# The delta rule's block products on one NeuronCore: 64x64 tiles against full 128x128 products over zero-padded operands

## The chip, the cores and the metric

The kernel runs on one core of a Trainium2 chip, as one program. The metric is the device time of one execution in microseconds; smaller is better. Times named here are medians of several executions, or parts of one profiled execution. The engines are called as the profile calls them: PE (TensorE, the matmuls), PEld (its weight loads), DVE (VectorE), ACT (ScalarE), POOL (GpSimd) and SP (SyncE, whose queue issues the DMAs here).

## What is computed

One layer of a streaming encoder over 2048 tokens of width 1024, in float32. One large input projection feeds two branches, a gated spatial mixing (group A) and a gated DeltaNet (group B) of 8 heads of width 128. Both go through one output projection, and a gated per-layer embedding follows. The part that matters here is the delta rule of group B, worked out in chunks of 64 tokens:

```python
def chunk_gated_delta_rule(q, k, v, g, beta):      # C = 64 tokens in a chunk
    ...
    A = where(strict, einsum('bhnik,bhnjk->bhnij', k_beta, k) * L, 0.0)
    T = triangular_solve(A + eye, eye)             # inverse of a 64x64 lower triangle
    u = einsum('bhnij,bhnjv->bhniv', T, v * beta[..., None])
    w = einsum('bhnij,bhnjk->bhnik', T, k_beta * exp(decay)[..., None])
    qk = einsum('bhnik,bhnjk->bhnij', q, k) * L
    ...
    def step(state, inp):                          # one chunk after another
        v_new = u_c - w_c @ state
        o_c = q_c @ state + qk_c @ v_new
        state = state * a_c + k_c.T @ v_new
        return state, o_c
```

## The kernel before

The tokens run in two passes of 1024. In each pass the projections are a stream of 128x512 products, each done as three float32r passes over operands split into a high and a low part (`mm3`). Everything else is woven into this stream by hand: an object `Flow` keeps an estimated time, and small tasks (generators) emit their instructions between the products of the stream when their estimates say that their inputs are ready. The result is one fixed order of instructions on each engine. `Flow` books a small float32 product by its moving width alone (`mm`), so its estimate is the same for 64 and for 128 partitions.

Group B goes head by head, 8 heads in each pass, numbered 0 to 15 in the text. A pair of two 64-token chunks stands on the 128 partitions, and is called a unit here; a head in a pass has 8 units in two blocks of 4. For each head and pass there are three stages.

- `front` builds the matrix `AT` (what `A` is in the reference, transposed) and `QK` from the products `pkq`, and writes the two diagonal 64x64 blocks of `AT` to DRAM (`atd`).
- `inverse` loads them in another layout (`ain`) and inverts all sixteen 64x64 triangles of a head at once on GpSimd, by 63 steps of a multiply (`xtmp`) and a subtract (`xs`). The result goes to DRAM (`td`) and comes back as `Dt`, in two DMAs (`d` = 0 and 1), one for each half of the partitions.
- `chain` walks through the 8 units. Each unit solves with the inverses in `Dt` in three products: the upper half (`Dt`), the coupling from the upper to the lower half (`AT`), and the lower half (`Dt`). These three are called block products here. Before the change they are on 64 partitions and 64 columns. Around them stand `pc<-S,kq`, `pc<-w,kd` and two `po` products, which are 128x128. `r`, `x1` and `w` are the steps between the products, on DVE, ACT and DVE.

`finish` closes each block of four units: its sum of squares `sso` goes to DVE and then, as a power, to GpSimd, in the same queue as the steps of the next head's inversion. There are two such instructions for each head.

All DMAs are issued by SP in one order. PE takes its instructions in order too, so a product that waits holds up everything behind it.

Of the kernel before, what the change touches and what calls it, by code (L numbers as in the profile page):

```python
"""Hybrid gMLP + gated DeltaNet trunk layer, float32, on one core.

Large products run as three float32r passes over operands split exactly into a
high and a low part; the delta rule, the spatial mixing and the transposes run
in plain float32.
"""
# [1 line left out]

# [11 lines left out]
P = 128  # L20
# [8 lines left out]


class Flow:
    """Emission order: a stream of large products with latency-bound work woven in.

    Times are estimates in nanoseconds; they only decide the order in which
    each engine's instructions are issued.
    """

    def __init__(self):
        self.t = 0.0
# [61 lines left out]
def trunk(tc, a, out):  # L101
# [67 lines left out]
    with ExitStack() as outer:  # L169
# [164 lines left out]
                fl.used["kq"] -= 4  # L334

        def inv_rms(xs):
            """1 / rms of every token, along the free axis on all partitions."""
            dg = gt("xs", "dg", [P, 4, P], 1)
            for i, (xt,) in enumerate(xs):
                yield from fl.room("act")  # L340
                yield from fl.take("acc")
                fl.give("acc")
                junk = gt("acc", "junk", [P, D], 3, BF16)
                ss = gt("ss1", "ss1", [P, 2], 4)
                r, f = rstd_of(gp, ss[:, :1], D, "rs1", act(junk, xt, AF.Square, accum_out=ss[:, :1]))
                yield f
                f = ts(dg[:, i], ident, r, None, ALU.mult, after=f)
            fl.used["kq"] -= 4
            yield f + 2000
            rb = bank("ch", "rb", [P, 512])  # L350
            f = mm(rb, ones, dg.rearrange("p a b -> p (a b)"), True, True)
            yield f
            return rb
# [39 lines left out]
            return ps  # L393

        def proj_both(X, ui, c, mid):
            """Both blocks share the pass over X, which frees its first parts sooner."""
            banks = []
            for b in range(2):
                yield pj_free
                fl.used["pj"] = fl.used.get("pj", 0) + 1  # L400
                banks.append(bank("pj", "pj", [P, 512]))
            cc = slice(c * P, c * P + P)
            for k in range(NK):
                hi, lo = W[ui, k // 2]
                for b in range(2):
                    yield from mm3(banks[b], hi[:, k % 2, cc], lo[:, k % 2, cc], X[k][0][:, b], X[k][1][:, b],
                                   k == 0, k == NK - 1)
                if k % 2:
                    fl.give("w")
                mid[k]()  # L410
            return banks
# [58 lines left out]
                fl.spawn(scalars(ab), 9000, 3)  # L470

        def v_unit(X, p, ui, n, stats):
            """Token major products; several token tiles share the pass over the weights."""
            fetch(ui + 1)
            rest = rest_w(ui + 1)
            ab = gt("ab", "ab", [P, 16, 8], 1) if n == 0 else None
            w = 256 if n else 272
            if n:
                groups = [((0, 1), "pj"), ((2, 3), "m"), ((4, 5), "pj"), ((6, 7), "m")]
            elif p == 0:  # L480
                groups = [((0, 1, 2, 3), "pm"), ((4, 5, 6, 7), "pm")]
            else:
                groups = [((0, 1, 2, 3), "pm"), ((4, 5), "pj"), ((6, 7), "m")]
            for group, where in groups:
                banks = []
                for i, t in enumerate(group):
                    tag = ("pj", "m")[i // 2] if where == "pm" else where
                    yield fl.free(tag)
                    fl.used[tag] = fl.used.get(tag, 0) + 1
                    banks.append((t, tag, bank(tag, "pv", [P, 512])))  # L490
                for k in range(NK):
                    if p == 0 and n == 0:
                        yield lambda: xready[group[0] // 4] > k
                    yield lambda: len(X) > k and (ui, k // 2) in W
                    hi, lo = W[ui, k // 2]
                    for t, tag, ps in banks:
                        tk = slice((t % 4) * P, (t % 4) * P + P)
                        yield from mm3(ps[:, :w], X[k][0][:, t // 4, tk], X[k][1][:, t // 4, tk],
                                       hi[:, k % 2, :w], lo[:, k % 2, :w], k == 0, k == NK - 1)
                    if group[-1] == 7:  # L500
                        if k % 2:
                            fl.give("w")
                        if k in rest:
                            rest[k]()
                for t, tag, ps in banks:
                    fl.spawn(v_post(p, ps, t, n, stats, ab, tag), 170, 1)
                if 3 in group:
                    next_w(ui + 1, 0)
# [160 lines left out]
            return f  # L669

        def decay(p, h, b, i):
            """exp of the summed decays between two tokens, zero above the diagonal, transposed."""
            beta, gh, gl, ex, ne = SC[p]
            cs = slice(h * 8 + b * 4, h * 8 + b * 4 + 4)
            while len(fronts) < i + b - 1 or len(Ls) < i + b:
                yield fl.t + 300
            R = []
            for gg in (gh, gl):
                yield from fl.take("R")
                yield from fl.room("pool", 800)  # L680
                r = gt("R", "R", [P, 4, P], 2, F32R)
                f = asel(r, gg[:, cs, None].bitcast(F32).to_broadcast([P, 4, P]))
                R.append(r)
            yield f
            yield from fl.take("m")
            pd = bank("m", "pd")
            mm(pd, mgt_r, R[0], True, False)
            f = mm(pd, mgt_r, R[1], False, True)
            fl.give("R")
            fl.give("R")  # L690
            yield f
            yield from fl.room("act")
            L = gt("L", "L", [P, 4, P], 2)
            f = act(L, pd, AF.Exp, after=f)
            fl.give("m")
            yield asel(L, L, after=f)
            Ls.append(L)
# [93 lines left out]
        def inverse(p, h, st):  # L791
# [31 lines left out]
            yield fl.t + 2600  # L823
            while len(done) < st["i"]:
                yield fl.t + 300
            Dt = gt("Dt", "Dt", [P, 8, 64], 1)
            for d in range(2):
                dma(Dt[d * 64:d * 64 + 64], td.rearrange("c (u d) i -> d c u i", d=2)[d])
            fl.spawn(chain(p, h, st, Dt), 4500, 0)

        def chain(p, h, st, Dt):
            beta, gh, gl, ex, ne = SC[p]
            while len(done) < st["i"] or len(st["R"]) < 2:
                yield fl.t + 300
# [1 line left out]
            for b in range(2):  # L836
# [4 lines left out]
                for u in range(4):  # L841
# [9 lines left out]
                        r = gt("r", "r", [P, P], 1)  # L851
                        yield stt(r, pc[:, 0], ne[:, cu], vn[:, u], ALU.mult, ALU.add, after=f)
                    po = bank("o", "po", [P, 2, P])
                    f = mm(pc[0:64, 1], Dt[0:64, b * 4 + u, :], r[0:64], True, True)
                    x1 = gt("x1", "x1", [64, P], 1)
                    fx = act(x1, pc[0:64, 1], AF.Copy, after=f)
                    if not first:
                        f = mm(po[:, 0], kq[:, u, 1, :], Sp, True, True)
                        oe = gt("oe", "oe", [P, P], 1)
                        fo = act(oe, po[:, 0], AF.Copy, scale=ex[:, 0, cu], after=f)  # L860
                    yield fx
                    f = mm(pc[64:128, 2], AT[0:64, u, 64:128], x1, True, True)
                    yield tt(r[64:128], r[64:128], pc[64:128, 2], ALU.subtract, after=f)
                    f = mm(pc[64:128, 1], Dt[64:128, b * 4 + u, :], r[64:128], True, True)
                    w = gt("w", "w", [P, P], 1)
                    yield ts(w, pc[:, 1], bn[:, u:u + 1], None, ALU.mult, after=f)
                    fs = 0
# [9 lines left out]
                    if first:  # L877
                        f = vcopy(ot[:, u], po[:, 1], after=f)
                    else:
                        f = tt(ot[:, u], oe, po[:, 1], ALU.add, after=max(f, fo))  # L880
                    junk = gt("junkc", "junkc", [P, P], 2, BF16)
                    f = act(junk, ot[:, u], AF.Square, accum_out=sso[:, u:u + 1], after=f)
                    yield fs
                fl.give("kq")
# [28 lines left out]
            tt(lo, src, hi.bitcast(F32), ALU.subtract)  # L913

        def stage(pool, j, name, loads, staged):
            """Two half tiles of 512 columns each, from the slots that are free by then."""
            if pool is gp and j % 3 == 2:
                tiles = []
                for _ in range(2):
# [16 lines left out]
            staged[j] = tiles  # L936

        def refill(pool, free, sources, sink, name):
            """Split operands into the resident slots as the products before release them."""
            n = len(sources)  # L940
            staged = {}
            for j in range(min(3, n)):
# [321 lines left out]
        nega = const("alog", [P, NH])  # L1264
        mgt_r = cp.tile([P, P], F32R, name="mgt_r")
        X0 = x_tiles()

        def setup():
            act(nega, nega, AF.Exp)
            ts(nega, nega, -1.0, None, ALU.mult)  # L1270
            act(mgt_r, mgt, AF.Copy)
# [72 lines left out]
```

## Time and profile before

| | us |
|---|---|
| median of 3 runs | 2430.47 |
| lowest and highest | 2428.53 and 2433.29 |
| span of the profiled execution | 2427.2 |
| PE busy in it | 2366.6 (98%) |
| GpSimd (POOL) busy in it | 1106.8 (46%) |
| DVE busy, ACT busy | 1310.7 (54%), 1023.5 (42%) |

The span runs from the first to the last instruction of the profiled execution, whose own whole time is not told apart from it; the median of the timed runs is 3.3 us above the span. A busy PE is not a PE at its peak: a product is counted from its start to its modelled end, and these overlap, so the distance from one start to the next tells more than a duration. A float32 product is shown as two passes.

### The profile page before, as it was taken

How to read it: one execution, taken by the hardware profiler on the slowest of the kernel's cores; microseconds unless marked ns; L12 is line 12 of the kernel's file. 1: busy time of each engine (PE TensorE's matmuls, PEld its weight loads, DVE VectorE, ACT ScalarE, POOL GpSimd, SP SyncE). 2: the span in 40 equal slices, each digit the busy share in tenths (PEclk: the TensorE clock that was granted, in tenths of full speed). 3: DMA queues.
4: the chain of work that ended last, by engine and by line, in shares of the span. 5: the costliest groups of instructions: out<-in, count | busy, mean ns of one | idle time of the engine just before them, and what ended most of it. 6: DMA issues, size and time to landing. Idle time of an engine off the chain costs nothing.

```text
span 2427.2 us, 34751 instructions
## 1 busy us (share of the span) xinstructions
PE 2366.6 (98%) x11884; PEld 1853.0 (76%) x11884; DVE 1310.7 (54%) x2843; ACT 1023.5 (42%) x2410; POOL 1106.8 (46%) x2246
## 2 busy tenths in 40 slices
PE   8999999999999999999999999999999999999998
PEld 8987677777776778987777676777766887887886
DVE  5456465565664754356556475564664334346665
ACT  5544354443543543444344353443532223234443
POOL 1128558567585681046757567576670000001111
PEclk9999999999999999999999999999999999999999
DMA  6532332223322242232232232322253457452221
GB/s 203 208 115 73 88 88 78 80 75 96 89 71 82 81 151 91 78 90 72 79 89 66 82 88 74 89 77 87 86 172 115 139 166 228 139 176 89 79 82 62
DMA packets 249201, 253.22 MB, mean 104 GB/s; under 512 B 66112, under 2 KB 163904, under 8 KB 249024
## 3 DMA queue, kind: packets, MB, share of 16 engines
q1 hardware_dynamic: 249024, 251.01, 33.1%
q8 instruction: 93, 1.52, 0.3%
q14 instruction: 84, 0.69, 0.1%
HBM read 195.89 MB, written 55.05 MB: 103 GB/s over the span
## 4 chain that ended last, share of the span: by engine, by line
PE 53%; POOL 31%; issue 6%; DMA 5%; DVE 2%; ACT 1%; SPq 0%; POOLq 0%; DVEq 0%; ACTq 0%
PE pj L115 16%; POOL xs L162 14%; POOL xtmp L162 13%; PE pso L115 12%; PE pg L115 7%; PE pv L115 7%; PE pc L115 5%; PE po L115 2%; PE pe L115 2%; POOL R L166 2%; DMA Dt<-td 1%; PE pkq L115 1%; DMA ain<-atd 1%; DMA td<-xs 1%; POOL sso L158 1%
## 5 line engine op out<-in xcount | busy, mean ns | idle before, releaser
L162 POOL TENSOR_TENSOR xtmp<-ain,xs 128x132 f32<-128x132 f32 (+47 forms) x1008 | 453.7, 450 | 344.8 <-DMA ain<-atd 260.8
L162 POOL TENSOR_TENSOR xs<-xs,xtmp 128x132 f32<-128x132 f32 (+47 forms) x1008 | 473.9, 470 | 79.0
L115 PE MATMUL pj<-xrhi,whi 128*128 128x512 f32 x768 | 314.5, 410 | 0.0
L115 PE MATMUL pj<-xhi,wlo 128*128 128x512 f32 x768 | 314.2, 409 | 0.0
L115 PE MATMUL pj<-xrhi,wlo 128*128 128x512 f32 x768 | 313.5, 408 | 0.0
L115 PE MATMUL pj<-xhi,whi 128*128 128x512 f32 x768 | 312.9, 407 | 0.0
L115 PE MATMUL pj<-xrlo,whi 128*128 128x512 f32 x768 | 312.5, 407 | 0.0
L115 PE MATMUL pj<-xlo,whi 128*128 128x512 f32 x768 | 311.2, 405 | 0.0
L158 POOL TENSOR_TENSOR rstd<-rstd,nhalf 128x1 f32<-128x1 f32 x64 | 42.9, 677 | 578.8 <-DVE rstd L146 578.8
L139 DVE SCALAR_TENSOR_TENSOR acc<-pre,cw,acc 128x512 f32<-128x512 f32 x288 | 226.4, 786 | 26.1 <-ACT acc L126 21.9
L115 PE MATMUL pso<-wohi,ylo 128*128 128x512 f32 x512 | 205.7, 402 | 0.0
L115 PE MATMUL pso<-wolo,yhi 128*128 128x512 f32 x512 | 204.5, 399 | 0.8 <-DVE wolo L135 0.7
L115 PE MATMUL pso<-wohi,yhi 128*128 128x512 f32 x512 | 202.5, 395 | 0.0
L135 DVE TENSOR_TENSOR wlo<-raw,whi 128x512 fp32r<-128x512 f32 x224 | 163.8, 734 | 63.5 <-ACT whi L126 60.6
L126 ACT ACTIVATE yhi<-yraw 128x512 fp32r<-128x512 f32 x128 | 80.2, 629 | 220.2 <-PE pso L115 216.3
L115 PEld LDWEIGHTS pj<-xhi,wlo 128*128 128x128 f32 x768 | 145.3, 189 | 31.9 <-issue 7.0
L115 PEld LDWEIGHTS pj<-xrhi,whi 128*128 128x128 f32 x768 | 145.6, 190 | 31.5 <-issue 7.5
L115 PEld LDWEIGHTS pj<-xhi,whi 128*128 128x128 f32 x768 | 145.5, 189 | 31.0 <-issue 6.9
L115 PEld LDWEIGHTS pj<-xrlo,whi 128*128 128x128 f32 x768 | 145.5, 189 | 30.4 <-issue 6.3
L115 PEld LDWEIGHTS pj<-xlo,whi 128*128 128x128 f32 x768 | 145.3, 189 | 30.7 <-issue 5.3
L115 PEld LDWEIGHTS pj<-xrhi,wlo 128*128 128x128 f32 x768 | 145.7, 190 | 29.5 <-issue 4.6
L126 ACT ACTIVATE junkc<-ot 128x128 bf16<-128x128 f32 x128 | 39.7, 310 | 302.9 <-DVE ot L135 283.7
(200 smaller groups left out, 4893.7 us busy)
## 6 DMA issues: line engine op xcount, KB each, us to landing
raw<-in_wu SPq DMA_DIRECT2D x224, 256.0 KB
ain<-atd SPq DMA_DIRECT2D x128, 256.0 KB
yraw<-ysc SPq DMA_DIRECT2D x128, 256.0 KB
vsc<-gv SPq DMA_DIRECT2D x64, 128.0 KB
gn<-vsc SPq DMA_DIRECT2D x32, 256.0 KB
ysc<-gn SPq DMA_DIRECT2D x32, 256.0 KB
ysc<-zb SPq DMA_DIRECT2D x32, 256.0 KB
wo<-in_wo SPq DMA_DIRECT2D x32, 256.0 KB
```

The costliest lines, as they stand in the source:

```text
L115: nc.tensor.matmul(o, lhsT, rhs, start=start, stop=stop)
L126: nc.scalar.activation(o, i, func, **kw)
L135: nc.vector.tensor_tensor(o, x, y, op)
L139: nc.vector.scalar_tensor_tensor(o, x, sc, y, op0, op1)
L158: nc.gpsimd.tensor_tensor(o, x, y, ALU.pow)
L162: nc.gpsimd.tensor_tensor(o, x, y, op)
L166: nc.gpsimd.affine_select(o, x, [[0, 4], [1, P]], ALU.is_ge, 0.0, 0, -1)
```

## The change

The three block products become full 128x128 products. `Dt` is now one tile of [128, 8, 128], made once and zeroed once; the DMAs fill only its two diagonal 64x64 blocks, so the off-diagonal blocks stay zero. `x1` is likewise one [128, 128] tile whose lower half stays zero. The first and the third block product both write all 128 rows of `pc[:, 1]`. Of the first, ACT uses only the upper half; the third gives both halves again, from the corrected `r`. The product with `AT` takes the whole matrix, and its lower half is used. Two scratch tiles are dropped: `oe`, whose content goes straight to `ot`, and `junkc`, which shares `junk`. The zeroing is two DVE instructions in `setup`.

```diff
         def inverse(p, h, st):
...
-            Dt = gt("Dt", "Dt", [P, 8, 64], 1)
             for d in range(2):
-                dma(Dt[d * 64:d * 64 + 64], td.rearrange("c (u d) i -> d c u i", d=2)[d])
-            fl.spawn(chain(p, h, st, Dt), 4500, 0)
+                dd = slice(d * 64, d * 64 + 64)
+                dma(Dt[dd, :, dd], td.rearrange("c (u d) i -> d c u i", d=2)[d])
+            fl.spawn(chain(p, h, st), 4500, 0)
...
                     po = bank("o", "po", [P, 2, P])
-                    f = mm(pc[0:64, 1], Dt[0:64, b * 4 + u, :], r[0:64], True, True)
-                    x1 = gt("x1", "x1", [64, P], 1)
-                    fx = act(x1, pc[0:64, 1], AF.Copy, after=f)
+                    f = mm(pc[:, 1], Dt[:, b * 4 + u], r, True, True)
+                    fx = act(x1[0:64], pc[0:64, 1], AF.Copy, after=f)
                     if not first:
                         f = mm(po[:, 0], kq[:, u, 1, :], Sp, True, True)
-                        oe = gt("oe", "oe", [P, P], 1)
-                        fo = act(oe, po[:, 0], AF.Copy, scale=ex[:, 0, cu], after=f)
+                        fo = act(ot[:, u], po[:, 0], AF.Copy, scale=ex[:, 0, cu], after=f)
                     yield fx
-                    f = mm(pc[64:128, 2], AT[0:64, u, 64:128], x1, True, True)
+                    f = mm(pc[:, 2], AT[:, u], x1, True, True)
                     yield tt(r[64:128], r[64:128], pc[64:128, 2], ALU.subtract, after=f)
-                    f = mm(pc[64:128, 1], Dt[64:128, b * 4 + u, :], r[64:128], True, True)
+                    f = mm(pc[:, 1], Dt[:, b * 4 + u], r, True, True)
...
-                        f = tt(ot[:, u], oe, po[:, 1], ALU.add, after=max(f, fo))
-                    junk = gt("junkc", "junkc", [P, P], 2, BF16)
+                        f = tt(ot[:, u], ot[:, u], po[:, 1], ALU.add, after=max(f, fo))
+                    junk = gt("junk", "junk", [P, P], 2, BF16)
...
+        Dt = gt("Dt", "Dt", [P, 8, P], 1)
+        x1 = gt("x1", "x1", [P, P], 1)
 
         def setup():
+            nc.vector.memset(Dt.rearrange("p u i -> p (u i)"), 0.0)
+            nc.vector.memset(x1, 0.0)
+            fl.op("dve", 1400)
```

No instruction changes its place on PE, ACT, POOL or SP, and DVE has the two zeroings more. What moves is a wait. On PE, at the first block product of head 0 (`vn` stands in for `r` there), the order before was the following; the names in brackets are the queues and engines waited for, and each of the two DMAs of `Dt` has a `DMAHW` name of its own.

```order
L115 MATMUL pj<-xhi,wlo 128x512
L115 MATMUL pc<-vn,Dt 64x128 [waits DMAHW6_49]
L115 MATMUL pj<-xhi,whi 128x512
L115 MATMUL pj<-xlo,whi 128x512
L115 MATMUL pj<-xhi,wlo 128x512
L115 MATMUL pc<-x_2912,AT 64x128 [waits Activation_49]
L115 MATMUL pj<-xhi,whi 128x512
L115 MATMUL pj<-xlo,whi 128x512
L115 MATMUL pj<-xhi,wlo 128x512
L115 MATMUL pc<-vn,Dt 64x128 [waits DMAHW7_49,DVE_49]
```

With the change the same rows read as follows.

```order
L115 MATMUL pj<-xhi,wlo 128x512
L115 MATMUL pc<-vn,Dt 128x128 [waits DMAHW7_49,DMAHW6_49]
L115 MATMUL pj<-xhi,whi 128x512
L115 MATMUL pj<-xlo,whi 128x512
L115 MATMUL pj<-xhi,wlo 128x512
L115 MATMUL pc<-x_218,AT 128x128 [waits Activation_49]
L115 MATMUL pj<-xhi,whi 128x512
L115 MATMUL pj<-xlo,whi 128x512
L115 MATMUL pj<-xhi,wlo 128x512
L115 MATMUL pc<-vn,Dt 128x128 [waits DVE_49]
```

The second DMA of `Dt` was waited for at the third block product, eight rows behind the first; now the first block product waits for both. The same holds at the first unit of every head.

## Rows read from the trace of the kernel before

**Rows 1.** The page: its first line, and shares of the chain that ended last.

```profile
span 2427.2 us, 34751 instructions
...
PE 53%; POOL 31%; issue 6%; DMA 5%; DVE 2%; ACT 1%; SPq 0%; POOLq 0%; DVEq 0%; ACTq 0%
```

**Rows 2.** PE groups by shape: busy us, mean ns, idle before (two passes per product).

```profile
L115 PE MATMUL pc<-r,Dt 64*64 64x128 f32 x480 | 103.4, 295 | 3.9 <-DMA Dt<-td 2.2 <-DVE acc L139 1.3 <-DVE kqlo L135 0.4
...
L115 PE MATMUL pc<-x,AT 64*64 64x128 f32 x256 | 54.9, 295 | 0.0
...
L115 PE MATMUL pc<-vn,Dt 64*64 64x128 f32 x32 | 7.1, 304 | 4.5 <-DMA Dt<-td 4.4
```

**Rows 3.** Timeline of SP's DMA issues between heads 4 and 5: start us, us, engine.

```profile
630.28 0.38 SPq L821 DMA_DIRECT2D td<-xs  x1
...
633.00 1.22 SPq L828 DMA_DIRECT2D Dt<-td  x2
642.07 1.26 SPq L761 DMA_DIRECT2D atd<-AT  x2
```

**Rows 4.** Timeline of PE after head 4's hand-over: block products, last pkq.

```profile
635.70 0.43 PE L115 MATMUL pc<-vn,Dt 64*64 64x128 f32 x2
...
638.41 0.43 PE L115 MATMUL pc<-vn,Dt 64*64 64x128 f32 x2
...
640.63 0.28 PE L115 MATMUL pkq<-kqhi,kqlo 128*128 128x256 f32 x1
```

**Rows 5.** Timeline, GpSimd's first step of head 5's inversion.

```profile
649.33 0.29 POOL L162 TENSOR_TENSOR xtmp<-ain,xs 128x63 f32<-128x63 f32 x1 [17.14 <-DMA ain<-atd]
```

**Rows 6.** Timeline of PE at head 5's hand-over.

```profile
734.28 0.43 PE L115 MATMUL pc<-vn,Dt 64*64 64x128 f32 x2 [0.32 <-DMA Dt<-td]
```

**Rows 7.** Waits of GpSimd inside head 4's inversion: us, times, longest.

```profile
POOL sso L158 <- DVE sso L139: 4.5, 2, 2.5
```

**Rows 8.** Timeline, a full-size product between stream products.

```profile
1875.51 0.40 PE L115 MATMUL pso<-wolo,yhi 128*128 128x512 f32 x1
...
1875.75 0.39 PE L115 MATMUL pc<-S,kq 128*128 128x128 f32 x2
...
1876.21 0.39 PE L115 MATMUL pso<-wohi,yhi 128*128 128x512 f32 x1
```

**Rows 9.** Timeline, a 64-partition product between stream products.

```profile
1879.19 0.40 PE L115 MATMUL pso<-wolo,yhi 128*128 128x512 f32 x1
...
1879.52 0.43 PE L115 MATMUL pc<-r,Dt 64*64 64x128 f32 x2
...
1880.21 0.39 PE L115 MATMUL pso<-wohi,yhi 128*128 128x512 f32 x1
```

**Rows 10.** Timeline, what one block product feeds: ACT copy, next block product.

```profile
1877.53 0.27 ACT L126 ACTIVATE x<-pc 64x128 f32<-64x128 f32 x1 [0.78 <-PE pc L115]
...
1878.25 0.43 PE L115 MATMUL pc<-x,AT 64*64 64x128 f32 x2
```

**Rows 11.** Waits of GpSimd, 250 to 928 us (inversions of heads 1 to 7).

```profile
POOL sso L158 <- DVE sso L139: 33.7, 13, 4.3
```

**Rows 12.** Waits of GpSimd, 1148 to 1830 us (inversions of heads 9 to 15).

```profile
POOL sso L158 <- DVE sso L139: 27.8, 10, 7.7
POOL sso L158 <- DMA gn<-vsc: 5.6, 2, 3.1
```

**Rows 13.** Timeline of PE at head 7's hand-over.

```profile
928.89 0.43 PE L115 MATMUL pc<-vn,Dt 64*64 64x128 f32 x2 [2.14 <-DMA Dt<-td]
```

**Rows 14.** Windows: busy time of each engine, granted clock, DMA share, GB/s.

```profile
924.00:930.40 6.40, 4.26 (x34) 3.58 (x32) 0.00 (x0) 0.81 (x3) 0.00 (x0) 1.00 0.65 198
930.50:933.90 3.40, 3.40 (x14) 2.85 (x15) 1.39 (x4) 0.00 (x0) 0.00 (x0) 0.50 0.22 77
```

**Rows 15.** Weight loads by tile pc: duration ns min/median/max.

```profile
L115 PEld LDWEIGHTS pc<-r,Dt x480: 129/132/228, 255.5 to 1879.6; 64*64 64x64 f32 x160
...
L115 PEld LDWEIGHTS pc<-S,kq x224: 186/189/192, 254.1 to 1875.8; 128*128 128x128 f32 x112
```

More of the change, by code (lines that the diff above doesn't have):

```diff
@@ L825, in inverse, with chain @@
                 yield fl.t + 300
-            Dt = gt("Dt", "Dt", [P, 8, 64], 1)
             for d in range(2):
-                dma(Dt[d * 64:d * 64 + 64], td.rearrange("c (u d) i -> d c u i", d=2)[d])
-            fl.spawn(chain(p, h, st, Dt), 4500, 0)
-        def chain(p, h, st, Dt):
+                dd = slice(d * 64, d * 64 + 64)
+                dma(Dt[dd, :, dd], td.rearrange("c (u d) i -> d c u i", d=2)[d])
+            fl.spawn(chain(p, h, st), 4500, 0)
+        def chain(p, h, st):
             beta, gh, gl, ex, ne = SC[p]
@@ L879, in chain @@
                     else:
-                        f = tt(ot[:, u], oe, po[:, 1], ALU.add, after=max(f, fo))
-                    junk = gt("junkc", "junkc", [P, P], 2, BF16)
+                        f = tt(ot[:, u], ot[:, u], po[:, 1], ALU.add, after=max(f, fo))
+                    junk = gt("junk", "junkc", [P, P], 2, BF16)
                     f = act(junk, ot[:, u], AF.Square, accum_out=sso[:, u:u + 1], after=f)
```

## The prediction

> **What bounds the kernel now.** I read the page first. PE holds 53% of the chain that ended last, and GpSimd holds 31% [rows 1], although PE is busy 98% of the span (the table above). The reader is to see that these two take turns: PE sets the pace, but some stretches are set by GpSimd's inversion. The groups of PE by shape show where they meet. PE's waits there are for `Dt`, 2.2 and 4.4 us [rows 2], so the inverses arrive about when PE wants them, seldom early. That is small today, and it is the point on which this forecast turns.
>
> So I followed one round in the timelines, from the first block product of head 4 to that of head 5; I call this moment the hand-over. PE starts head 4's first block product at 635.70 and the last `pkq` product of head 5's front at 640.63, 4.9 us later, with three block products on the way (the rows show the first and the last of them) [rows 4]. SP issues `atd` at 642.07 [rows 3]. GpSimd starts head 5's inversion at 649.33, released by the landing of `ain` [rows 5], 13.6 us after the hand-over. PE's next hand-over is at 734.28, after a wait of 0.32 us for `Dt` [rows 6]. The end of the round is seen one head earlier: `td` is issued at 630.28, the two `Dt` DMAs from 633.00 on [rows 3], and the product that needs the first of them starts at 635.70 [rows 4], 5.4 us after `td`. The round takes 98.6 us: 13.6 up to the inversion, 5.4 at its end, some 79.6 of inversion between.
>
> GpSimd is not busy for all of those 79.6 us. Inside one inversion it stood 4.5 us in two waits for DVE's `sso` [rows 7]. That `sso` belongs to the chain of the previous head, which PE is still working through: a queue of GpSimd that looks independent of PE waits for it twice in each head.
>
> **What a block product costs now, and after.** There are 480 and 32 passes with `Dt` and 256 with `AT` [rows 2], two to a product, so 384 block products, 24 in each of 16 heads. I take their price from starts, since durations overlap. Between two stream products, a product on 64 partitions takes 1879.19 to 1880.21, 1.02 us for two stream products and itself [rows 9]. A 128x128 product in the same place takes 1875.51 to 1876.21, 0.70 us [rows 8]. The difference, 0.32 us, is empty time around the 64-partition product: the next stream product, and the block product itself, start late. The full product has the same two passes over 128 columns, so I take the row of `pc<-S,kq` as the price of the new products. PE's gain, if nothing else bound, is 384 x 0.32 = 123 us, 7.7 us a head.
>
> Does the dependent work fit the shorter distance? ACT's copy for the `AT` product starts at 1877.53 and takes 0.27, so ends at 1877.80; the product that reads it starts at 1878.25 [rows 10]. Of these 0.45 us the change takes 0.32, and 0.13 stay. It is thin, and bounds the cost of new waits: nothing where the row repeats, and some tenths of a us in a head where ACT or DVE is held up. I take nothing, since PE gets spare time at each hand-over (below) that would hide it.
>
> **Around a hand-over** four things change; each round has one of each, and there are 14 rounds (7 in each pass).
> - The stretch up to the last `pkq` has three block products [rows 4]: 3 x 0.32 = 1.0 us less.
> - The `sso` waits. The first follows block 0 of the previous head (12 block products, 3.8 us earlier), the second follows block 1 (24, 7.7 us earlier); the inversion itself starts 1.0 earlier. Each wait is 2 to 3 us (4.5 in two, the longer 2.5 [rows 7]), so both go. All of them come to 33.7 us in pass 1 [rows 11] and 27.8 + 5.6 in pass 2 [rows 12] (the profile puts the 5.6 down to a DMA, but it is the same instruction), 67.1 in all, 4.8 a round. Bounds: nothing, and the whole; I take the whole, as 2.8 us (3.8 less 1.0) is more than the 2.5 of the row.
> - The first block product now waits for both `Dt` DMAs. SP takes 1.22 us to issue the two [rows 3], so the second is 0.6 us later: +0.6. In the old order the second was needed at 638.41 [rows 4], and the products between covered it; that cover is gone. Queued behind the waiting product is all of PE's stream.
> - The clock. The loop shortens by less than PE does, so PE will stand at the hand-over. It stood 2.14 us at head 7's [rows 13], and afterwards the granted clock was 0.50, the 1.2 GHz level, from 930.5 to 933.9, and 1.00, 2.4 GHz, until then [rows 14]. 3.4 us at half speed lose 1.7 us of PE work, and they lie between the hand-over and the last `pkq` (4.9 us), thus on the path. Bounds: 0 and 1.7. I take 1.7, since the new wait comes out longer than 2.14.
>
> Per round: -1.0 - 4.8 + 0.6 + 1.7 = -3.5 us; 14 rounds give -49. PE alone would be 7.7 - 1.7 = 6.0 us quicker in a round, so it waits 2.5 us more than today for `Dt`, 3 us a round and some 40 in all. That agrees with the clock falling.
>
> Outside the rounds PE sets the pace, and two heads gain in full: head 7's chain runs under the projections of the second pass, head 15's under the output projection, with no inversion to wait for. 2 x 7.7 = 15.4 us.
>
> The rest is at nothing. The two zeroings (1.4 us by the kernel's own booking, once) stand on DVE, 54% busy, early, hundreds of instructions ahead of the first chain. The `Dt` DMAs move the same bytes in runs of 64 numbers, as `td` holds them. `oe` into `ot` and `junkc` into `junk` change no duration; ACT's write to `ot` now waits for the transposes of the block before, which stand ahead in PE's order. If a cover failed, each would be under 2 us.
>
> **Sum:** 67.1 + 14.0 - 8.4 - 23.8 + 15.4 = 64.3 us less. The profiled span of 2427.2 becomes 2363; the runs' median is 3.3 above that span, so I forecast **2366**.
>
> **Rivals.**
> - *PE keeps everything.* If the loop were shorter than I read it (a later part of the chain, not `Dt`, placing the hand-over), all 123 us come: 2307. For it: PE waits for `Dt` only 6.6 us in all today [rows 2]. Against it: these waits are short because both were level, and the end of the round (5.4 us from `td` to product) has no slack in it. Chance 0.10, from 2300 to 2330.
> - *The loop gets nothing back.* If GpSimd's `sso` waits last because `sso` is late for another reason (DVE's or ACT's own queues), a round changes by 0.6 + 1.7 - 1.0 = +1.3 us, 14 of them +18, less 15.4: 2433, no change. For it: the wait that the profile puts down to a DMA [rows 12]. Against it: the waits follow the chain's end, head after head. 0.05; halfway between this and the forecast, 2396 to 2425, another 0.03.
> - *The full product is dearer* (the slower side). Its weights have 128 columns: the load takes 188 ns where the 64-column one takes 132 [rows 15]. If the 56 ns stood on PE's path, 768 loads would cost 43 us and the gaps [rows 9] would be of the waits, not of the tile: 2430.5 + 43 = 2474. It decides when the stretch with a full product is longer than 1.02 us. Against it: the row of 0.70 has these very loads in it, overlapped. 0.03. The Trainium skill speaks for it in two places. "TensorE: Matmul & The Clock Gate", in "LDWEIGHTS (loading the stationary operand)", has a load's time go by its columns, so half for 64; in "Part 3: Packing small matmuls — row/col tiling" it advises small products to use part of the array, for concurrency. By that rule a wider product would be a step back. The trace agrees on the loads, 132 against 188, but here no second tile runs beside the first, and the starts favour the full product; I go by these.
>
> **How the numbers follow.** The forecast case has 0.79. Its own bounds: without the clock's fall 24 us less, 2342; some more gain from GpSimd's other waits on PE, 2330; half of the `sso` relief missing, 33 more, 2399. I give **2330 to 2396** for 8 in 10: about 0.1 below it, 0.1 above. A measurement of this kernel can tell about 0.2% (5 us) from no change. Faster 0.79 + 0.10 + 0.03 = **0.92**, same **0.05**, slower **0.03**.
>
> **What would show it.** (1) Stream, block product, two stream products: 0.70 us, no empty PE time around the block product. (2) GpSimd's waits for `sso` near 0 in both stretches. (3) PE's wait for `Dt` near 40 us, at some 14 hand-overs. (4) The granted clock at 0.50 shortly after most of them. (5) Rounds near 95 us, heads 7 and 15 some 8 shorter each. The prediction is wrong if (3) is small, which leads to 2307, or if (2) stays, which leads to 2433.

## The result and the profile after

The change makes the kernel faster: 2355.4 us median (4 runs, 2353.73 to 2356.76) against 2429.5 of before (4 runs, 2425.43 to 2433.29), a ratio of 0.9696 with a 95% interval of 0.9682 to 0.971. That is 74 us less; the forecast was 64 less, at 2366. The profiled execution's span is 2352.0 after and 2427.2 before [rows 1], 75.2 less.

The page of the changed kernel, its first line, the busy times, and the shares of the chain that ended last:

```profile
span 2352.0 us, 34693 instructions
...
PE 2269.4 (96%) x11884; PEld 1877.0 (80%) x11884; DVE 1312.9 (56%) x2845; ACT 1013.6 (43%) x2410; POOL 1113.1 (47%) x2246
...
PE 45%; POOL 38%; DMA 7%; issue 5%; DVE 2%; ACT 1%; SPq 1%; POOLq 0%; DVEq 0%; ACTq 0%
```

PE fell from 53% of that chain to 45%, GpSimd rose from 31% [rows 1] to 38%: the loop over the inversion sets more of the span than before.

The timeline of PE after head 4's hand-over (start us, us, engine, line, operation). It has the first block product, the second one between stream products, and the last `pkq` of head 5's front; the next hand-over follows:

```profile
625.29 0.46 PE L115 MATMUL pc<-vn,Dt 128*128 128x128 f32 x2
...
626.06 0.40 PE L115 MATMUL pj<-xhi,wlo 128*128 128x512 f32 x1
626.30 0.38 PE L115 MATMUL pc<-x,AT 128*128 128x128 f32 x2
626.44 0.48 PE L115 MATMUL pj<-xhi,whi 128*128 128x512 f32 x1
626.75 0.39 PE L115 MATMUL pj<-xlo,whi 128*128 128x512 f32 x1
...
629.43 0.28 PE L115 MATMUL pkq<-kqhi,kqlo 128*128 128x256 f32 x1
...
718.99 0.49 PE L115 MATMUL pc<-vn,Dt 128*128 128x128 f32 x2 [1.13 <-DMA Dt<-td]
```

From the `pj` ahead of the block product to the second `pj` behind it, it is 626.06 to 626.75, 0.69 us; it was 1.02 [rows 9]. The front's last `pkq` comes 4.1 us after the hand-over; it came 4.9 after [rows 4].

The same round on SP's queue, after:

```profile
618.86 0.38 SPq L821 DMA_DIRECT2D td<-xs  x1
...
621.59 1.22 SPq L828 DMA_DIRECT2D Dt<-td  x2
...
712.63 0.38 SPq L821 DMA_DIRECT2D td<-xs  x1
```

SP's `td` of the same round in the kernel before, and GpSimd's first step after:

```profile
728.73 0.38 SPq L821 DMA_DIRECT2D td<-xs  x1
```

```profile
638.17 0.29 POOL L162 TENSOR_TENSOR xtmp<-ain,xs 128x63 f32<-128x63 f32 x1 [16.15 <-DMA ain<-atd]
```

The reader can split the round as the prediction did. From the hand-over to the inversion: 625.29 to 638.17, 12.9 us (13.6 before). The inversion: 638.17 to 712.63, 74.5 (649.33 [rows 5] to 728.73 before, 79.4). From `td` to the product: 712.63 to 718.99, 6.4 (728.73 to 734.28 [rows 6] before, 5.6). Together 93.7 us against 98.6. The prediction took the end of the round from one head earlier, 5.4 us, and so had 79.6 for the inversion; the end of that head is now 618.86 to 625.29, 6.4.

The waits of GpSimd inside head 4's inversion (543 to 618.5 us: total, times, longest), complete:

```profile
POOL xtmp L162 <- DMA ain<-atd: 19.7, 1, 19.7
POOL iv L158 <- DVE bn L144: 0.7, 1, 0.7
```

The two waits for `sso` [rows 7] are gone. In the long stretches of [rows 11] and [rows 12], two and three `sso` waits are left. Up to the hand-overs of heads 7 and 15 they are one of 0.2 and one of 0.7 us, where 67.1 us stood before. The others, up to 27.2 us long, lie behind these two hand-overs, where no inversion is held up by them.

The waits of PE, after:

```profile
PE pd L115 <- POOL R L166: 23.7, 26, 2.8
PE pkq L115 <- DVE kqlo L135: 18.9, 21, 3.6
PE pc L115 <- DMA Dt<-td: 14.2, 9, 3.0
```

The same view of the kernel before, which was not among the rows above:

```profile
PE pkq L115 <- DVE kqlo L135: 20.6, 23, 3.1
PE pd L115 <- POOL R L166: 8.2, 10, 1.6
PE pc L115 <- DMA Dt<-td: 6.5, 8, 2.1
```

PE's spare time didn't gather at the hand-over alone, where `Dt` is waited for (7.7 us more); the wait for the mask `R`, which GpSimd makes in the same queue as the inversion, grew most (by 15.5 us).

The first block products of heads 0, 7, 8 and 15, first after, then before, let the whole span be split:

```profile
253.66 0.38 PE L115 MATMUL pc<-vn,Dt 128*128 128x128 f32 x2
...
905.33 0.46 PE L115 MATMUL pc<-vn,Dt 128*128 128x128 f32 x2 [2.99 <-DMA Dt<-td]
...
1115.95 0.40 PE L115 MATMUL pc<-r,Dt 128*128 128x128 f32 x2
...
1764.57 0.46 PE L115 MATMUL pc<-r,Dt 128*128 128x128 f32 x2 [2.18 <-DMA Dt<-td]
```

```profile
249.74 0.43 PE L115 MATMUL pc<-vn,Dt 64*64 64x128 f32 x2
...
1148.37 0.43 PE L115 MATMUL pc<-r,Dt 64*64 64x128 f32 x2
...
1832.53 0.40 PE L115 MATMUL pc<-r,Dt 64*64 64x128 f32 x2 [1.41 <-DMA Dt<-td]
```

With head 7's 928.89 of before [rows 13]: the seven rounds of pass 1 took 679.2 us and take 651.7; those of pass 2 took 684.2 and take 648.6. That is 63.1 less in 14 rounds, 4.5 each. Head 7's part up to head 8 went from 219.5 to 210.6 (8.9 less), head 15's up to the end from 594.7 to 587.4 (7.3 less). Head 0's hand-over comes 3.9 us later. 63.1 + 8.9 + 7.3 - 3.9 gives the 75.2, within rounding.

### The profile page after: what moved, and what is told of

The parts are those of the page before. It is cut to its first block, busy times and chain, and to the rows that moved or that the text cites. A ratio compares the mean times of both kernels' runs of the same rounds, so it can differ in the third digit from the quotient of the medians.

```text
span 2352.0 us, 34693 instructions
## 1 busy us (share of the span) xinstructions
PE 2269.4 (96%) x11884; PEld 1877.0 (80%) x11884; DVE 1312.9 (56%) x2845; ACT 1013.6 (43%) x2410; POOL 1113.1 (47%) x2246
## 4 chain that ended last, share of the span: by engine, by line
PE 45%; POOL 38%; DMA 7%; issue 5%; DVE 2%; ACT 1%; SPq 1%; POOLq 0%; DVEq 0%; ACTq 0%
POOL xs L162 17%; POOL xtmp L162 16%; PE pso L115 12%; PE pj L115 11%; PE pg L115 7%; PE pv L115 7%; DMA ain<-atd 3%; PE pc L115 2%; PE pe L115 2%; POOL R L166 2%; POOL sso L158 1%; PE pkq L115 1%; DMA Dt<-td 1%; DMA atd<-AT 1%; DMA td<-xs 1%
## 5 line engine op out<-in xcount | busy, mean ns | idle before, releaser
L115 PEld LDWEIGHTS pj<-xlo,whi 128*128 128x128 f32 x768 | 146.9, 191 | 25.4
L135 DVE TENSOR_TENSOR ylo<-yraw,yhi 128x512 fp32r<-128x512 f32 x128 | 89.7, 702 | 137.3 <-ACT yhi L126 135.0
L126 ACT ACTIVATE whi<-raw 128x512 fp32r<-128x512 f32 x224 | 140.3, 627 | 60.4 <-PE pj L115 39.7
```

What stands on the lines that cost most here:

```text
L115: nc.tensor.matmul(o, lhsT, rhs, start=start, stop=stop)
L126: nc.scalar.activation(o, i, func, **kw)
L135: nc.vector.tensor_tensor(o, x, y, op)
```

## The experiments

Four theories stand behind the expectations. A is the prediction's own: each small block product costs PE some 0.3 us of empty time, and the loop over GpSimd takes part of the saving back. B: before the change the loop alone set the pace, and what the change saved is the `sso` waits. C: the rest of PE's saving is lost in the dependent steps of the chain, not in the loop. D, formed later: DVE's queue holds up the fronts.

### Is the price PE's? The inversion cut in half

Both kernels do 32 of the 63 steps of the inversion, so their inverses are unfinished; all products stay.

```diff
-            for j in range(63):
+            for j in range(32):
...
-                if jj == 7 and jc < 6:
+                if jj == 7 and jc < 2:
```

For the kernel before:

> The kernel before with the inversion cut to its first 32 of 63 steps (the inverses are left unfinished; GpSimd's part of a round falls from some 79 us to about 42). Theory A (64-partition products cost 0.32 us of empty PE time each, and GpSimd's inversion holds the hand-over only level with PE): PE sets the whole pace, so little changes, 2415 to 2430 us. Rival B (GpSimd's inversion alone sets the rounds): 14 rounds shorten by tens of us, under 2200. Rival C (PE's own chain steps set the pace, GpSimd never does): 2425 to 2430.

For the changed kernel:

> The changed kernel with the same cut (the inverses are left unfinished). Theory A: with GpSimd out of the way the full gain on PE shows: 100 to 123 us under the cut kernel before, so some 2300 to 2325. Rival C (the 75 us seen are all that PE can give, the rest of the 123 being new waits inside a unit): 75 us under the cut kernel before, about 2350.

Measured: 2393.95 us (0.9849 of before, 0.9832 to 0.9866) and 2284.72 (0.9412, 0.9397 to 0.9428), on one chip. The difference is 109 us, in the 100 to 123 of A and far from C's 75. The kernel before gained 36 us from the cut, more than A had expected. The page of the changed kernel with the cut:

```profile
PE 2245.4 (98%) x11884; PEld 1867.0 (82%) x11884; DVE 1263.0 (55%) x2845; ACT 988.9 (43%) x2391; POOL 645.0 (28%) x1254
```

PE is at 98%, and GpSimd is busy 28% of the span. So the full products are worth 109 us where PE alone decides, 0.28 us for each of the 384; and the loop cost 36 us before (2430 - 2394) and 71 after (2355 - 2285). The difference between the two, 35 us, is what the loop took back. (The cut changes the estimates of `Flow` and with them the order, in both kernels alike: PE has the same order in the two cut kernels.)

### Was GpSimd's queue alone the bound before?

`sso` goes through a reciprocal on DVE and no longer through a power on GpSimd (so the norm is another one).

```diff
-            yield power(sso, sso, nhalf[:, :4], after=f)
+            f = recip(sso, sso, after=f)
```

> The kernel before with the power of sso taken off GpSimd: DVE takes a reciprocal of it instead (so the norm of the delta rule's output is another one). GpSimd's inversion loses its 4.8 us of waits and 2 us of work a round. Theory A: GpSimd and PE were level, so PE, still slowed by its 64-partition products, keeps the pace: 0 to 10 us less, 2420 to 2430. Rival B (the sso wait was what paced the rounds, and its end is the gain): 14 x 4.8 to 6.8 us less, 2335 to 2365.

Measured: 2420.14 us, 0.9966 (0.9954 to 0.9979), 10 us less. B falls: with the `sso` waits gone from GpSimd, little came of it, and with the inversion cut, where B had under 2200, it was 2394. GpSimd's waits moved instead: over the whole span those for `ain` grew from 260.8 to 306.0 us, those of `L` for ACT from 25.4 to 63.6. (Both edits change `Flow`'s estimates and PE's order, so the 10 and the 36 us aren't exact prices.) The `sso` relief by itself is worth little; it pays together with a quicker PE.

### What the second DMA of `Dt` costs

The changed kernel without the second of the two DMAs (the lower inverses stay zero).

```diff
-            for d in range(2):
+            for d in range(1):
                 dd = slice(d * 64, d * 64 + 64)
```

> The changed kernel without the second DMA of Dt (the inverses of the lower chunks are left out and stay zero), so the first block product waits for one DMA. Theory A: the wait for the second DMA stands on the loop of the rounds, 0.6 to 1.0 us each: 8 to 14 us less than the changed kernel, 2341 to 2347. Rival C (PE sets the pace after the change): 0 to 2 us.

Measured: 2344.2 us, 0.9654 (0.9641 to 0.9667), 11 us below the changed kernel: 0.8 us a round over 14. Added up over the 14 rounds, the time from `td` to the hand-over is 94.5 us in the changed kernel and 86.0 here: 8.5 of the 11, or 0.6 a round, lie in the stretch where the DMA is waited for.

### What makes a small product dear: its rows, or that it is not the whole array

In the changed kernel with the inversion cut, only the first `Dt` product is narrowed to 64 columns; it keeps its 128 partitions, and loads half as many columns of weights.

```diff
-                    f = mm(pc[:, 1], Dt[:, b * 4 + u], r, True, True)
+                    f = mm(pc[0:64, 1], Dt[:, b * 4 + u, 0:64], r, True, True)
```

> The changed kernel with the inversion cut as in the two cut kernels (inverses left unfinished), and one product in three (the first with Dt) narrowed from 128 to 64 columns of weights, still on all 128 partitions. Drain theory (a product on a part of the array costs empty time, whichever way it is cut): 128 x 0.32 = 41 us over the cut changed kernel (2284.7), some 2320 to 2330. Load theory (what counts is the time of the weight load, 132 ns for 64 columns against 188): 14 us under it, 2270. A third way (only a cut in partitions costs): 2284.

Measured: 2317.28 us (0.954, 0.9519 to 0.9561), 32.6 above the kernel with the cut alone: 0.25 us for each of the 128 products, on the side of the empty time and against the rule by the load. The timeline of PE, and the weight load of the product (PEld), with the narrow product and then with the full one, each between a `pj` and `po<-S,kq`:

```profile
608.09 0.40 PE L115 MATMUL pj<-xlo,whi 128*128 128x512 f32 x1
608.41 0.19 PEld L115 LDWEIGHTS pc<-r,Dt 128*64 128x64 f32 x2 [0.36 <-DVE pre L150]
608.41 0.43 PE L115 MATMUL pc<-r,Dt 128*64 128x128 f32 x2
608.77 0.49 PE L115 MATMUL po<-S,kq 128*128 128x128 f32 x2
```

```profile
609.69 0.39 PE L115 MATMUL pj<-xhi,whi 128*128 128x512 f32 x1
609.83 0.30 PEld L115 LDWEIGHTS pc<-r,Dt 128*128 128x128 f32 x2 [0.18 <-DVE r L139]
609.92 0.40 PE L115 MATMUL pc<-r,Dt 128*128 128x128 f32 x2
610.16 0.39 PE L115 MATMUL po<-S,kq 128*128 128x128 f32 x2
```

The narrow product begins 0.32 us after `pj` and the next follows 0.36 later; with the full one both distances are 0.23 and 0.24. Time is lost on both sides of the narrow product. The weight load shows how: the full product's starts 0.09 us ahead of the product, while `pj` still runs; the narrow one's starts only with the product itself, at 608.41. (The row puts that down to DVE's `pre`, but it ended at 608.22, 0.19 us earlier; with the full product the load starts 0.05 us after DVE's `r` has ended at 609.78.) Over all 128 products the medians of the two distances are 0.33 and 0.36 with the narrow product, 0.23 and 0.23 with the full one. The 64x64 products of before begin as late: 1879.19 to 1879.52 is 0.33 [rows 9]. The Trainium skill has a sentence on this, in "TensorEngine Tiling (Array Packing)", "Key Properties": "Changing tiling mode (not just tile) drains the TensorE". The rows agree in kind; the price of 0.25 to 0.28 us is these runs' own.

### Is the gain linear in the products?

The kernel before with the product with `AT` alone made full, over a zero-padded `x1`.

```diff
+                    fx = act(x1[0:64], pc[0:64, 1], AF.Copy, after=f)
...
-                    f = mm(pc[64:128, 2], AT[0:64, u, 64:128], x1, True, True)
+                    f = mm(pc[:, 2], AT[:, u], x1, True, True)
...
+        x1 = gt("x1", "x1", [P, P], 1)
...
+            nc.vector.memset(x1, 0.0)
```

> The kernel before with one product in three made full (that with AT, over a zero-padded x1); both products with Dt stay on 64 partitions. Theory A (before the change PE and GpSimd are level, and GpSimd holds only after the first gains): the first third earns most of what it saves, up to 128 x 0.32 = 41 us: 2390 to 2405, more than a third of the 75 us. Linear share (each product earns the same in the end): 25 us, 2405. Rival B (GpSimd alone sets the rounds): under 15 us, over 2415.

Measured: 2388.59 us, 0.9832 (0.9818 to 0.9847), 40 us less, all that a third of the products can give at 0.32. So it is not linear: the first 128 products earn 40 us, the other 256 only 33. B had under 15 here, and PE's order is the one of before. The waits of GpSimd between 250 and 928 us:

```profile
POOL sso L158 <- DVE sso L139: 15.2, 13, 2.3
```

Of the 33.7 us [rows 11] half are still there. The 14 rounds became 37 us shorter, and 32 of these lie in the inversions: it is by way of `sso` that PE's saving reaches the loop. Up to here PE and the loop shorten together, and only beyond it does the loop fall behind. Of what the other 256 don't earn, 8.5 to 11 us are the second DMA of `Dt` (by the run without it), which the first product waits for only once it is full.

### The second `Dt` DMA from another queue

```diff
-                dma(Dt[dd, :, dd], td.rearrange("c (u d) i -> d c u i", d=2)[d])
+                (dma, nc.scalar.dma_start)[d](Dt[dd, :, dd], td.rearrange("c (u d) i -> d c u i", d=2)[d])
```

> The changed kernel with the second DMA of Dt issued by ACT's queue beside the first on SP's. Theory A (the second issue stands on the loop): 0.6 us a round, 8 us less than the changed kernel, some 2347, if ACT reaches the issue in time. Rival: ACT stands at the issue until td has landed, up to 2.7 us in each head, and the units' copies behind it are late: 0 to 20 us more, 2355 to 2375.

Measured: 2381.51 us, 0.9798 (0.9781 to 0.9815), 26 us above the changed kernel, past the rival's range. The timeline of ACT, and a wait of PE:

```profile
621.13 0.53 ACTq L828 DMA_DIRECT2D Dt<-td  x1
621.71 0.60 ACT L126 ACTIVATE pre<-pj 128x512 f32<-128x512 f32 x1 [2.42 <-DMA td<-xs]
```

```profile
PE pkq L115 <- ACT kqhi L126: 15.0, 9, 3.3
```

ACT stands at the issue until `td` has landed, everything behind it is late, and PE waits for ACT's `kqhi`, a wait that the changed kernel doesn't have.

### Taking the masks off GpSimd

After the change GpSimd's `R` holds PE up for 23.7 us, so both masks (`R` and `L`) went to DVE as products with a triangle of ones, in the changed kernel and in the one before.

```diff
-        nc.gpsimd.affine_select(o, x, [[0, 4], [1, P]], ALU.is_ge, 0.0, 0, -1)
-        return fl.op("pool", 570, after)
+        return tt(o, x, uincl[:, None, :].to_broadcast([P, 4, P]), ALU.mult, after=after)
...
-                yield from fl.room("pool", 800)
+                yield from fl.room("dve")
```

In the changed kernel:

> The changed kernel with the triangular masks of the decays (six affine selects a head on GpSimd, 5 us inside an inversion) made by DVE as products with a triangle of ones. Theory A (GpSimd's inversion holds the rounds after the change): rounds 3 to 5 us shorter, and PE's wait for R (23.7 us) nearly gone: 30 to 65 us less, 2290 to 2325. Rival C (PE and its chain steps hold them): only the wait for R, 2335 to 2350, or more where DVE's 4 us a head more are in the way.

In the kernel before:

> The same masks on DVE in the kernel before. Theory A (before the change PE, with its empty time, is level with GpSimd): PE keeps the pace, so only waits go, 10 to 25 us less, 2405 to 2420, a third or less of what the masks bring to the changed kernel. Rival B (GpSimd alone held the rounds before): as much as in the changed kernel, 30 to 65 us.

Measured: 2374.0 us (0.977, 0.9753 to 0.9786), 19 above the changed kernel, and 2447.2 (1.0071, 1.0056 to 1.0085), 18 above the one before. The figures of both expectations fail, and on the wrong side; only the open end of rival C ("or more where DVE's 4 us a head more are in the way") has room for the first. PE's waits of the first:

```profile
PE pkq L115 <- DVE kqlo L135: 57.6, 16, 4.7
PE po_t L121 <- DVE ot L135: 8.5, 6, 3.4
PE pc L115 <- DMA Dt<-td: 8.5, 5, 4.6
```

The wait for `R` is gone, and one three times as long as before for `kqlo` on DVE has come. That is where theory D comes from. The next kernel moves the `R` masks alone:

> The changed kernel with only the masks of R (four affine selects a head, 3.4 us inside an inversion) made by DVE; those of L stay on GpSimd, so DVE waits for no product and no exp ahead of kqlo, which held up the kernel with all masks on DVE (its PE waited 57.6 us for kqlo). Theory A (GpSimd's inversion holds the rounds): rounds some 3 us shorter and the wait for R (23.7 us) gone from PE: 25 to 50 us less than the changed kernel, 2305 to 2330. Rival D (any work moved to DVE ahead of kqlo costs at the front what it saves in the inversion): 2350 or more.

Measured: 2369.38 us, 0.9753 (0.9738 to 0.9769), 14 above the changed kernel, as D had it. The timeline of DVE and of PE there shows a chain at work:

```profile
609.05 0.18 DVE L154 RECIPROCAL bn<-bn 128x4 f32<-128x4 f32 x1 [5.49 <-POOL iv L158]
609.26 0.16 DVE L135 TENSOR_TENSOR bn<-bn,beta 128x4 f32<-128x4 f32 x1
609.34 0.73 DVE L135 TENSOR_TENSOR kqlo<-kq,kqhi 128x512 fp32r<-128x512 f32 x1
```

```profile
610.12 0.58 PE L115 MATMUL pkq<-kqlo,kqhi 128*128 128x256 f32 x1 [5.29 <-DVE kqlo L135]
```

The reciprocal overwrites `bn`, which GpSimd's `iv` has still to read, and `iv` stands in the queue among the steps of the inversion. DVE stands 5.49 us, `kqlo` comes behind it, and PE stands 5.29 us. (`Flow`'s estimates and PE's order changed too, so the 14 us aren't all shown to be this chain's.) Over the 14 rounds the inversions took 15 us less than in the changed kernel, so the loop did get its relief; the stretches from the hand-over to the inversion took 25 more, and those from `td` to the hand-over 13 more.

### The front without that wait

The reciprocal writes another tile than the one that `iv` reads, in the changed kernel (the scratch tile `junk`, which `junkc` shares, has one buffer in place of two, for room):

```diff
+            sq_ = gt("sqe", "sqe", [P, 4], 2)
...
-            f = ts(bn, ss[:, 0:4], EPS, None, ALU.add)
-            fiv = power(iv, bn, phalf[:, :4], after=f)
+            f = ts(sq_, ss[:, 0:4], EPS, None, ALU.add)
+            fiv = power(iv, sq_, phalf[:, :4], after=f)
...
-            recip(bn, bn)
+            recip(bn, sq_)
```

> The changed kernel, in the same order of instructions, with one wait taken away: the front's reciprocal writes another tile than the one that GpSimd's power iv reads, so DVE no longer stands at it until GpSimd has come to iv (48.1 us of DVE's waits in the changed kernel). Theory A in its widened form (any instruction of GpSimd that stands among the inversion's steps and that DVE or PE waits for holds the rounds): PE's wait for kqlo (18.9 us) falls to under 5 and the last pkq comes earlier: 5 to 20 us less than the changed kernel, 2335 to 2350. Rival (these waits are covered by the wait for Dt, which grows by as much): 2353 to 2358.

Measured: 2356.33 us (2352.37 to 2362.36), 0.9697 (0.9679 to 0.9715), no change. PE's waits:

```profile
PE pc L115 <- DMA Dt<-td: 36.3, 15, 4.2
PE pd L115 <- POOL R L166: 21.0, 25, 2.8
```

The wait for `kqlo`, 18.9 us, has left the list; the one for `Dt` grew from 14.2 to 36.3. PE saved time in the front and stood longer at the hand-over, so the loop holds the rounds, as the rival had it.

The same edit on top of the `R` masks on DVE:

> The kernel with the masks of R on DVE (2369.4) with the same wait taken away. If the 54.0 us that its PE waited for kqlo come from DVE standing at iv, they go, and the 3.4 us a head that the masks save GpSimd show at last: 2300 to 2335. If DVE's added work is what holds up kqlo (rival D), 2355 to 2370.

Measured: 2393.67 us, 0.9855 (0.9841 to 0.9869), 24 above the masks alone; the expectations all miss. PE's waits:

```profile
PE pc L115 <- DMA Dt<-td: 82.9, 16, 7.2
...
PE pkq L115 <- DVE kqlo L135: 1.5, 1, 1.5
```

The wait for `kqlo` is gone but for 1.5 us, and 82.9 us for `Dt` stand in its place. The order of the fronts isn't what parts this kernel from the one with the masks alone: every engine has the same order in the two. A window (columns as in the last section) around head 4's hand-over at 627.65, where PE stood 7.21 us, shows one thing that does:

```profile
625.40:632.10 6.70, 4.45 (x14) 3.81 (x15) 1.47 (x5) 2.22 (x9) 0.59 (x1) 0.50 0.23 52
```

The granted clock is 0.50 at or right behind the hand-over in 13 of the 14 rounds here. Over the 14 rounds the stretches from the hand-over to the inversion took 14 us more than with the masks alone, the inversions 25 more, and those from `td` to the hand-over 14 less. The clock bears on the first; why the inversions became longer is open. No kernel that computes the reference was faster than the changed one.

## Why the prediction was right

The direction and the mechanism hold, and the time lies in the stated range, 11 us below the forecast. One term was badly sized, and others were off in the other direction. Added up over all 14 rounds, from the same starts as in the round above (a minus is time saved):

| | before | after | change | forecast |
|---|---|---|---|---|
| hand-over to inversion | 171.1 | 162.7 | -8.4 | -14.0 + 23.8 |
| inversion | 1106.4 | 1043.1 | -63.3 | -67.1 |
| `td` to hand-over | 85.8 | 94.5 | +8.6 | +8.4 |

- **The block product.** Forecast 0.32 us each from two pairs of starts [rows 8, 9], 123 in all. The timeline shows 0.69 us for the stretch forecast at 0.70, and the pair with the cut inversion gives 109 us in the whole, 0.28 each.
- **PE keeps everything (2307)** is refuted: the changed kernel stands 71 us above what it reaches with half the inversion.
- **The full product is dearer (2474)** is refuted by sign, and the narrow product shows that its halved load buys nothing. (The prediction's 188 ns for the full load is 189 in its row [rows 15]; nothing hangs on it.)
- **The `sso` waits.** Forecast 4.8 us a round, all gone. They are gone inside the inversions but for 0.9 us in all, and the inversions took 4.5 us a round less. "The loop gets nothing back" is refuted with that.
- **The front stretch.** Forecast 1.0 us less; the last `pkq` moved from 4.9 to 4.1, 0.8.
- **The second `Dt` DMA.** Forecast +0.6 from SP's issue time. In the round above it is +0.8, one head earlier +1.0, over all 14 rounds 0.6 each.
- **The clock, the step that failed.** The prediction said: "I take 1.7, since the new wait comes out longer than 2.14", for all 14 rounds, 23.8 us. The granted clock was at 0.50 right behind 2 of the 14 hand-overs, those of heads 3 and 10. There the price was near the forecast: after head 3's the last `pkq` came 5.7 us behind the hand-over where 4.1 is usual, 1.6 more. But the kernel before, which the prediction took to be free of it, had two falls in these places too, around head 9's hand-over and behind head 10's (0.50 from 1237.7 to 1241.1 and from 1343.5 to 1346.9; hand-overs at 1239.14 and 1341.41). The first row of the table has the term together with the front stretch: 8.4 us less, where the forecast's two terms make 9.8 more. Against 0.8 to 1.0 us a round for the products alone, 3 to 6 us are left for the clock, net of the falls of before, not 23.8.
- **PE's spare time.** Forecast as a wait for `Dt` of some 40 us at 14 hand-overs; it was 14.2 at 9. By the prediction's own sign a small wait should have led to 2307, and it did not. PE's idle time (span less busy time) rose by 22.0 us, from 60.6 to 82.6: 15.5 of it for `R` and 7.7 for `Dt`. The rest fits the clock, by falls that lie mostly between the hand-overs: its mean is 0.993 before and 0.987 after, which makes 17 and 31 us of full-speed time lost in the two spans, 14 more (an estimate). With the 22.0 that is about the 35 that the loop took back. The run with the other `bn` tile has 36.3 us for `Dt`, but the wait for `kqlo` that it does away with, 18.9 us, is in them; it doesn't bear out the forecast's amount.
- **Heads 7 and 15.** Forecast 15.4 us; 16.2 measured.
- **Head 0,** not in the forecast: its hand-over comes 3.9 us later. PE waited 3.6 us there for `kqlo`, at 242.5, and the granted clock was 0.50 from 241.4 to 248.2.
- **The dropped scratch tiles,** taken at nothing, have no run of their own.

The measured terms add up: 63.3 + 8.4 - 8.6 + 16.2 - 3.9 = 75.4, the 75.2 of the spans within rounding. Against the forecast's 64.3, the front stretch with the clock gives 18.2 more; the inversion gives 3.8 less, head 0 takes 3.9, and the others are within 1. That the forecast came so near is in part luck: without the clock's term it would have been 2342, 13 us too low, so the term stood in for losses that the prediction didn't see.

## What to carry to other kernels

A product that uses part of the array, alone among full ones, can cost more than the full product over zeros: compare the starts of the neighbours on both sides, not the durations. Price such a change twice, once with PE alone as the bound and once by the loop of the other engine that runs at the same pace; here the first third of the edit earned 40 us and the rest 33, as the loop became the bound on the way and took on a wait of its own (the second `Dt` DMA). Here a wait of PE that was taken away (the `kqlo` wait) only moved to the place where the loop is waited for. And add up each term over all rounds, in both kernels: one round, or one kernel alone, misled on the DMA and on the clock.

## What the hardware showed that was not expected

The length of a stand did not tell whether the clock fell. In the changed kernel PE stood 2.99 us for `Dt` at 905.3, and the granted clock stayed at 1.00, the 2.4 GHz level; after 1.59 us at 528.1 it was 0.50, 1.2 GHz:

```profile
528.10:531.50 3.40, 3.40 (x11) 2.81 (x12) 0.46 (x2) 2.36 (x5) 0.00 (x0) 0.50 0.00 0
905.30:911.00 5.70, 5.67 (x45) 5.48 (x45) 2.26 (x7) 1.63 (x7) 0.00 (x0) 1.00 0.14 47
```

These are rows of two windows (length, busy time of PE, PEld, DVE, ACT, POOL, granted clock, DMA share, GB/s). In the kernel with the other `bn` tile a stand of 2.52 us at 619.4 was followed by 1.00 and one of 2.30 us at 712.3 by 0.50. In the kernel with the `R` masks on DVE and the other `bn` tile, by contrast, there was a fall in 13 of 14 rounds, with stands of 3.0 to 7.2 us, and none at head 7's hand-over, after 3.02. One row of such a fall [rows 13, 14] is therefore no ground for counting on one in every round, nor its absence for counting on none.

The other surprise is the 128x64 product. It has all 128 rows and half the columns, and it loses 0.25 us where the 64x64 product loses 0.28: of these two shapes the smaller part costs hardly more. No run here has several part products in a row, so whether the price is that of the part or of the change to it and back isn't shown.
